# Reordering the first two tiles of a hybrid convolution and attention block

## The chip, the cores and the metric

The kernel runs on one core of one Trainium2 chip. The metric is the device time of one execution in microseconds (us), as the median of several runs; a separate execution is profiled. The core has five engines that each work through a queue of their own in order: PE (TensorE, matrix products; PEld is its weight load), DVE (VectorE), ACT (ScalarE), POOL (GpSimd) and SP (SyncE, which here issues nearly all DMAs).

## What is computed

One encoder layer over 4096 tokens of width 1024. A normalised input is projected by one large weight `w_in`; half of the columns feed a gated short convolution, the other half feed attention with three dilated windows, whose results are mixed and gated; a last projection is added to the input.

```python
h = rmsnorm(x, norm_w)
proj = jnp.einsum('bsd,de->bse', h, w_in)            # 1024 -> 4096
u, g_b, g_c, z_conv, q, k, v, z_attn = jnp.split(proj, splits, axis=-1)   # 512 columns each
y_conv = short_gated_conv(u, g_b, g_c, conv_w, conv_b) * jax.nn.silu(z_conv)
q = rmsnorm(q.reshape(b, s, ATTN_HEADS, HEAD_DIM), q_norm_w)
k = rmsnorm(k.reshape(b, s, ATTN_HEADS, HEAD_DIM), k_norm_w)
...   # three dilated windows, softmax over their log-sum-exps
y_attn = o.reshape(b, s, ATTN_WIDTH).astype(x.dtype) * jax.nn.silu(z_attn)
x = x + jnp.einsum('bse,ed->bsd', jnp.concatenate([y_conv, y_attn], axis=-1), w_out)
```

## The kernel before

The first stage, up to about 754 us, computes q, k, v and the attention gate z for 32 tiles of 128 tokens. Later stages do the convolution, the attention and the last projection. Products are exact to more than 16 bits: each operand is held as a high and a low half-precision part, and one product is three matmuls (high by high, high by low, low by high, lines 385 to 387).

The weights of q, k, v and z are the groups 4, 5, 6 and 7 of `w_in`, 512 columns each, held as 8 row blocks (kt) of 128 by 512. They arrive in float32 (`raw`) and are made into parts in the kernel, group by group:

- `w_square` (line 258, ACT) squares a block and sums each row; `w_scale` (lines 260 to 282) adds the eight sums, lets PE add across the partitions (line 264), takes an inverse root on POOL (line 267) and leaves one scale for the group;
- `w_split` writes the high part on ACT (line 286) and the low part on DVE (line 287).

Tokens go through `stats1` and `stats2` (the root mean square: ACT, POOL, then four small DVE steps) and then either `x_transpose` (PE turns the tile, lines 352 to 360) or `x_split` (parts on ACT and DVE, then two transposing DMAs issued by SP, lines 366 to 369). Before the change tiles 0, 1 and 2 take the first way, all others the second.

The first two tiles go together: `mm((0, 1), bank, group)` runs 48 matmuls, six for each row block. Functions given to `mm` by row block are issued between its matmuls, and that is where the squares, scales and splits of the next group stand, together with the later work on q and k: `post_qk1` (squares on ACT, sum on DVE, inverse root on POOL) and `post_qk2` (four small DVE steps, one or two products on DVE, a high part on ACT, a low part on DVE). `v_sums` adds the absolute values of v's weights (eight ACT steps and eight matmuls), `v_scales` and `v_gate` make factors of them that `post_v` and `post_z` need. From tile 2 on the loop `for t in range(2, NT)` handles one tile at a time; the order of the source is the order of every queue. Results of PE lie in eight banks; a bank can be written again when its last reader is done.

Of the kernel before, what the change touches and what calls it, by code (L numbers as in the profile page):

```python
# [65 lines left out]
def tile_hybrid_block(  # L66
# [39 lines left out]
    def bank(n, shape, dt=F32):  # L106
        return ps.tile(shape, dt, name=f"bank{n % 8}")
# [148 lines left out]
    def w_square(cg, kt, src):  # L256
        sq = pa.tile([128, D], F16, name="xsq")[:, 0:512]
        nc.scalar.activation(sq, src, AF.Square, scale=nwc[:, kt:kt + 1], accum_out=wss[:, cg, kt:kt + 1])

    def w_scale(cg):  # L260
# [12 lines left out]
        if cg in (4, 5):  # L273
            mul = 1.0 if cg == 4 else QK_SCALE
            c = rqs[:, cg - 4]
            nc.vector.tensor_scalar(c[:, 1:2], i, -0.5 * mul, None, op0=OP.mult)
            nc.vector.tensor_scalar(c[:, 2:3], i, 1.5 * mul, None, op0=OP.mult)
            nc.vector.tensor_scalar(c[:, 0:1], i, i, 1.0 / DH, op0=OP.mult, op1=OP.mult)
        if cg == 1:
            nc.vector.tensor_tensor(i, i, inv[:, 3:4], op=OP.mult)  # L280
        if cg in (3, 7):
            nc.vector.tensor_scalar(cz[:, cg // 4:cg // 4 + 1], i, 0.5, None, op0=OP.mult)

    def w_split(hi, lo, src, cg, kt):
# [4 lines left out]
    def group_steps(cg):  # L289
        def spl(kt):  # L290
            w = wa[(cg - 4) * 8 + kt]
            w_split(w[:, 0], w[:, 1], raw.pop((cg, kt)), cg, kt)
        return ([lambda kt=kt: w_square(cg, kt, raw[cg, kt]) for kt in range(KT)], [lambda: w_scale(cg)],
                [lambda kt=kt: spl(kt) for kt in range(KT)])

# [39 lines left out]
    def stats1(t):  # L335
        sq = pa.tile([128, D], F16, name="xsq")
        ss = pa.tile([128, 1], F32, name="ssx", bufs=2)
        nc.scalar.activation(sq, XT[t], AF.Square, accum_out=ss)
        RX[t] = rsqrt1(ss, 1, 1.0 / D, "x")

    def stats2(t):
        RX[t] = rsqrt2(RX[t], -0.5 * H_SCALE, 1.5 * H_SCALE)

    def h_views(t):
        c = t // 2
        b = (hb[c] if t % 2 else h_room(c, c % 3))[:, t % 2]
        HT[t] = (b[:, 0], b[:, 1])
        return HT[t]

    def x_transpose(t, b0=4):  # L350
        hi, lo = h_views(t)
        nc.vector.tensor_scalar(XT[t], XT[t], RX.pop(t), None, op0=OP.mult)
        for g in range(2):
            p = bank(b0 + g, [128, 4, 128])
            for k in range(4):
                kt = 4 * g + k
                nc.tensor.transpose(p[:, k, :], XT[t][:, kt * 128:(kt + 1) * 128], identf)
            s = slice(4 * g, 4 * g + 4)
            nc.scalar.activation(hi[:, s], p, AF.Copy)
            nc.vector.tensor_tensor(lo[:, s], p, hi[:, s], op=OP.subtract)  # L360
# [14 lines left out]
    def h_store(c):  # L375
        nc.sync.dma_start(hT_d[c], hb.pop(c).rearrange("p a b k n -> p (a b k n)"))
# [68 lines left out]

    vs = pa.tile([128, 512], F32, name="vs")

    def v_sums():
        pcs = bank(7, [128, 512])
        for n in range(KT):  # L450
            a = pa.tile([128, 512], F16, name="wk", bufs=3)
            nc.scalar.activation(a, wa[16 + n][:, 0], AF.Abs)
            nc.tensor.matmul(pcs, ones16, a, start=n == 0, stop=n == KT - 1)
        nc.vector.tensor_scalar(vinv, pcs, 1e-30, None, op0=OP.max)

    def v_scales():
# [49 lines left out]
        nc.vector.tensor_scalar(cvec, cq[:, 2, :], cm[:, 1:2], QK_SCALE, op0=OP.mult, op1=OP.mult)  # L506


    steps = {cg: group_steps(cg) for cg in (4, 5, 6, 7)}
    cq = pa.tile([128, 3, DH], F32, name="cq")  # L510
    nc.sync.dma_start(cq[:, 0, :], dap(q_norm_w, 0, [[0, 128], [1, DH]]))
    nc.sync.dma_start(cq[:, 1, :], dap(k_norm_w, 0, [[0, 128], [1, DH]]))
    stats1(0)
    stats1(1)
    stats2(0)
    stats2(1)
    x_transpose(0, 4)
    x_transpose(1, 6)
    for part in steps[4]:
        run_tasks(part)  # L520

    def with_steps(cg, more=None):
        sq, fin, spl = steps[cg]
        out = {kt: [] for kt in range(KT)}
        for kt in range(4):
            out[kt] += sq[2 * kt:2 * kt + 2]
        out[3] += fin
        for kt in range(4):
            out[4 + kt] += spl[2 * kt:2 * kt + 2]
        for kt, tasks in (more or {}).items():  # L530
            out[kt] += tasks
        return out

    pq = mm((0, 1), 0, 4, with_steps(5), 4)
    pk = mm((0, 1), 2, 5, with_steps(6, {
        0: [lambda: post_qk1(0, "q", pq[0])], 1: [lambda: post_qk1(1, "q", pq[1])], 2: [gains],
        5: [lambda: post_qk2(0, "q")], 7: [lambda: post_qk2(1, "q")]}))
    pv = mm((0, 1), 4, 6, with_steps(7, {
        0: [lambda: post_qk1(0, "k", pk[0]), lambda: qk_store(0, "q")], 1: [lambda: post_qk1(1, "k", pk[1])],
        2: [lambda: qk_store(1, "q"), v_sums], 3: [lambda: stats1(2)], 4: [v_scales, lambda: stats2(2)],  # L540
        5: [lambda: post_qk2(0, "k"), lambda: x_transpose(2, 0)], 6: [lambda: post_qk2(1, "k")], 7: [v_gate]}))
# [728 lines left out]
```

## Time and profile before

| | us |
|---|---|
| median of 3 runs (2233.95 to 2235.58) | 2235.02 |
| the profiled execution, its own time | 2230.64 |
| its span in the trace | 2228.8 |
| PE busy | 2109.8 (95% of the span) |
| DVE busy | 1432.0 (64%) |
| ACT busy | 1085.4 (49%) |

A row of the trace gives the start, the duration, the engine, the line, the operation and its operands, and in brackets how long the engine had sat idle and what ended that. Matmuls overlap, so the distance of two starts tells the pace, not the duration.

### The profile page before, as it was taken

The numbers are of one execution on the slowest core, as the hardware profiler recorded it, in microseconds if no ns is written. First come the engines' busy times: TensorE is split into PE (matmuls) and PEld (weight loads), VectorE is DVE, ScalarE is ACT, GpSimd is POOL, SyncE is SP. The second block draws the span as 40 slices with busy tenths as digits, with TensorE's granted clock in tenths as the row PEclk, the third lists the DMA queues.
The fourth block names the chain that finished last, engine by engine and source line by source line (L and its number), as shares of the span: only waits on it lengthen the run. The fifth ranks groups of instructions, "written<-read, shape, count | busy, mean of one in ns | idle before, by whom it ended". The sixth has DMA issues, their size and how long they took to land. (4 is left out here: it accounts for less than half of the span.)

```text
span 2228.8 us, 48736 instructions
## 1 busy us (share of the span) xinstructions
PE 2109.8 (95%) x17726; PEld 1559.6 (70%) x17726; DVE 1432.0 (64%) x4009; ACT 1085.4 (49%) x3128; POOL 844.9 (38%) x1635
## 2 busy tenths in 40 slices
PE   5699999999999989999999999999999899999999
PEld 2244444444444678888888898888888797788887
DVE  4655665655656346766666666676666676787776
ACT  6423333333333146766666666666666675222221
POOL 1123322232323255532554335553353354343332
PEclk9799999999999999999999999999999999999999
DMA  5155567775565586678865897668966458687775
GB/s 181 71 142 161 162 169 162 184 191 154 146 176 153 157 160 156 141 155 182 168 157 117 166 193 167 152 158 170 180 154 144 124 119 224 204 269 241 243 244 185
DMA packets 625006, 377.83 MB, mean 170 GB/s; under 512 B 401281, under 2 KB 567292, under 8 KB 618620
## 3 DMA queue, kind: packets, MB, share of 16 engines
q1 hardware_dynamic: 503396, 304.19, 55.1%
q10 hardware_dynamic: 121368, 70.53, 12.5%
q8 instruction: 139, 2.28, 0.4%
q14 instruction: 103, 0.84, 0.1%
HBM read 174.54 MB, written 110.39 MB: 128 GB/s over the span
## 5 line engine op out<-in xcount | busy, mean ns | idle before, releaser
L809 PE MATMUL bank<-hb,w 128*128 128x256 f16 x2048 | 559.9, 273 | 0.1
L810 PE MATMUL bank<-hb,w 128*128 128x256 f16 x2048 | 559.9, 273 | 0.0
L811 PE MATMUL bank<-hb,w 128*128 128x256 f16 x2048 | 559.8, 273 | 0.0
L387 PE MATMUL bank<-wa,hb 128*128 128x512 f16 x1024 | 392.5, 383 | 6.0 <-DMA hb<-xs 6.0
L385 PE MATMUL bank<-wa,hb 128*128 128x512 f16 x1024 | 393.0, 384 | 2.1 <-ACT wa L286 2.1
L386 PE MATMUL bank<-wa,hb 128*128 128x512 f16 x1024 | 392.5, 383 | 0.2 <-DVE wa L287 0.2
L1013 DVE CUSTOM_DVE_ANT_0 L<-bank,bt,alpha 128x256 f32<-128x256 f32 (+1 forms) x768 | 319.2, 453 | 106.9 <-PE bank L1001 79.3
L1022 ACT ACTIVATE L<-L,ot 128x256 f32<-128x256 f32 (+1 forms) x768 | 363.6, 476 | 25.9 <-DVE ot L1013 24.7
L238 POOL TENSOR_TENSOR rs_rq<-rs_mq,mhalf 128x8 f32<-128x8 f32 x64 | 107.8, 1684 | 301.1 <-DVE rs_mq L237 301.1
L974 POOL COPY qz<-qk 64x128 f16<-64x128 f16 x512 | 158.4, 309 | 161.3 <-PE bank L1001 143.9
L811 PEld LDWEIGHTS <-w 128*128 128x128 f16 x2048 | 201.0, 98 | 23.7
L810 PEld LDWEIGHTS <-w 128*128 128x128 f16 x2048 | 201.0, 98 | 22.2 <-issue 0.3
L809 PEld LDWEIGHTS <-w 128*128 128x128 f16 x2048 | 201.0, 98 | 19.8
L1057 DVE SCALAR_TENSOR_TENSOR pt<-bank,pt 128x512 f16<-128x512 f32 x192 | 132.6, 691 | 118.9 <-ACT pt L1045 118.5
L1045 ACT ACTIVATE pt<-bank 128x512 f16<-128x512 f32 x192 | 114.6, 597 | 169.0 <-PE bank L1039 163.8
L387 PEld LDWEIGHTS <-hb 128*128 128x128 f16 x1024 | 101.1, 99 | 132.6 <-DMA hb<-xs 8.9
L1076 PE MATMUL bank<-vt,pt 128*128 128x64 f16 x1536 | 175.7, 193 | 19.2 <-DMA pt<-src 16.6
L1061 DVE SCALAR_TENSOR_TENSOR src<-L,src 128x384 f16<-128x384 f32 (+1 forms) x192 | 131.2, 683 | 92.0 <-ACT src L1051 85.6
L385 PEld LDWEIGHTS <-hb 128*128 128x128 f16 x1024 | 102.1, 100 | 124.3 <-issue 7.2
L386 PEld LDWEIGHTS <-hb 128*128 128x128 f16 x1024 | 101.2, 99 | 124.2 <-issue 7.4
L1077 PE MATMUL bank<-vt,pt 128*128 128x64 f16 x1536 | 175.9, 193 | 0.0
L1078 PE MATMUL bank<-vt,pt 128*128 128x64 f16 x1536 | 175.9, 193 | 0.0
(197 smaller groups left out, 4478.4 us busy)
## 6 DMA issues: line engine op xcount, KB each, us to landing
hb<-hT SPq DMA_DIRECT2D x32, 1024.0 KB, 5.6
o_d<-ot ACTq DMA_DIRECT2D x32, 528.0 KB, 5.1
qk<-o_d SPq DMA_DIRECT2D x63, 264.0 KB, 3.6
hT<-hb SPq DMA_DIRECT2D x16, 1024.0 KB, 4.1
wst<-in_w_in_dram SPq DMA_DIRECT2D x64, 256.0 KB, 2.8
qk<-in_x_dram SPq DMA_DIRECT2D x32, 512.0 KB
qk_d<-h SPq DMA_DIRECT2D x128, 96.0 KB, 3.6
vt<-v_d ACTq DMA_DIRECT2D x48, 256.0 KB, 4.2
```

Of the source, the lines that this page charges most:

```text
L385: nc.tensor.matmul(p, hi[:, kt, :], w[:, 0], start=kt == 0, stop=False)
L386: nc.tensor.matmul(p, hi[:, kt, :], w[:, 1], start=False, stop=False)
L387: nc.tensor.matmul(p, lo[:, kt, :], w[:, 0], start=False, stop=kt == KT - 1)
L809: nc.tensor.matmul(pt, w_h, hi[:, :, kt], start=kt == 0, stop=False)
L810: nc.tensor.matmul(pt, w_h, lo[:, :, kt], start=False, stop=False)
L811: nc.tensor.matmul(pt, w_l, hi[:, :, kt], start=False, stop=kt == KT - 1)
L974: nc.gpsimd.tensor_copy(QZ[u % QZB][i][half], cols(q_t[i], U["qc"], half))
L1013: nc.vector.tensor_tensor_reduce(out=L[:, i], in0=p[i][:, 0:kn], in1=bias[:, U["b0"]:U["b0"] + kn], scale=alpha, scalar=BIG, op0=OP.add, o ...
L1022: nc.scalar.activation(L[:, i], L[:, i], AF.Exp, scale=-1.0, bias=ot[:, b, i, DH:DH + 1], accum_out=ot[:, b, i, DH + 1:DH + 2])
L1076: nc.tensor.matmul(p[:, i], hi, v[:, 0:DH], start=j == 0, stop=False)
L1077: nc.tensor.matmul(p[:, i], hi, v[:, DH:], start=False, stop=False)
L1078: nc.tensor.matmul(p[:, i], lo, v[:, 0:DH], start=False, stop=j == 1)
```

## The change

All that moves lies in the first stage's work on tiles 0, 1 and 2. The scale of each group is now made from four squares on ACT and four maxima of absolute values on DVE (`square`, `w_max`) in place of eight squares, and three short DVE steps join them. The squares of the next group stand between the splits of the present one. The work of tiles 0 and 1 on q and k stands behind all splits, in the matmuls of z; so do the absolute values of v's weights, into tiles of their own, while the matmuls that add them stand behind q of tile 2, in bank 1. Tile 2 goes the way of the later tiles, by transposing DMAs. z of tiles 0 and 1 goes to the banks 6 and 7.

```diff
+    def w_max(cg, kt, src):
+        nc.vector.tensor_reduce(wss[:, cg, kt:kt + 1], src, axis=AX.X, op=OP.max, apply_absolute_value=True)
+    def w_scale(cg, maxima=0):
+        if maxima:
+            t = wss[:, cg, KT - maxima:]
+            nc.vector.tensor_tensor(t, t, nwc[:, KT - maxima:], op=OP.mult)
+            nc.vector.tensor_tensor(t, t, t, op=OP.mult)
...
+    def square(cg, n):
+        w_square(cg, n, raw[cg, n])
+        w_max(cg, n + 4, raw[cg, n + 4])
...
     stats1(0)
+    stats2(0)
+    xp0 = x_transpose(0, 4)
     stats1(1)
-    stats2(0)
+    x_parts(0, xp0)
     stats2(1)
-    x_transpose(0, 4)
-    x_transpose(1, 6)
-    for part in steps[4]:
-        run_tasks(part)
+    xp1 = x_transpose(1, 6)
+    for n in range(4):
+        square(4, n)
+        if n == 1:
+            x_parts(1, xp1)
+    w_scale(4, 4)
...
+    def parts(cg):
+        out = [each(spl, cg, kt) for kt in range(KT)]
+        if cg < 7:
+            for n, at in enumerate((3, 5, 7, 9)):
+                out.insert(at, each(square, cg + 1, n))
         return out
+    run_tasks(parts(4))
+    pq = mm((0, 1), 0, 4, {5: [each(w_scale, 5, 4)], 7: parts(5)})
+    pk = mm((0, 1), 2, 5, {5: [each(w_scale, 6, 4)], 7: parts(6)})
+    pv = mm((0, 1), 4, 6, {5: [each(w_scale, 7, 4)], 7: parts(7) + [
+        each(stats1, 2), gains, each(post_qk1, 0, "q", pq[0]), each(stats2, 2)]})
     load_x(3)
     load_x(4)
+    pz = mm((0, 1), 6, 7, {
+        0: [each(x_split, 2)], 1: [each(post_qk2, 0, "q"), each(post_qk1, 1, "q", pq[1])],
+        2: [each(qk_store, 0, "q"), v_abs], 3: [each(post_qk2, 1, "q"), each(post_qk1, 0, "k", pk[0])],
+        4: [each(qk_store, 1, "q"), each(stats1, 3)], 5: [each(post_qk2, 0, "k"), each(post_qk1, 1, "k", pk[1])],
+        6: [each(qk_store, 0, "k"), each(stats2, 3)], 7: [each(post_qk2, 1, "k"), each(h_store, 0)]})
...
     pq = mm((2,), 0, 4)[0]
+    qk_store(1, "k")
+    v_sums()
+    v_scales()
+    post_v(0, pv[0])
+    post_v(1, pv[1])
+    v_gate()
     post_z(0, pz[0])
     post_z(1, pz[1])
```

The removed calls of `mm` had the same matmuls, with squares, scale and splits of the next group at fixed row blocks and the work on q, k and v in between.

ACT before, at the end of the squares of v's weights (`w_191` and the like are blocks of raw weights, `wa_..` their parts, `h_..` the parts of q, `wk` a scratch tile):

```order
L258 ACTIVATE xsq,wss<-w_195,nwc 128x512
L258 ACTIVATE xsq,wss<-w_197,nwc 128x512
L286 ACTIVATE wa_125<-w_183,nws 128x512
L286 ACTIVATE wa_126<-w_185,nws 128x512
L286 ACTIVATE wa_127<-w_187,nws 128x512
L286 ACTIVATE wa_128<-w_189,nws 128x512
L416 ACTIVATE h_531<-wk 128x4x2x64
L286 ACTIVATE wa_129<-w_191,nws 128x512
```

ACT after the change, in the second half of the splits of k's weights:

```order
L295 ACTIVATE wa_119<-w_170,nws 128x512
L258 ACTIVATE xsq,wss<-w_183,nwc 128x512
L295 ACTIVATE wa_120<-w_172,nws 128x512
L258 ACTIVATE xsq,wss<-w_185,nwc 128x512
L295 ACTIVATE wa_121<-w_174,nws 128x512
L258 ACTIVATE xsq,wss<-w_187,nwc 128x512
L295 ACTIVATE wa_122<-w_176,nws 128x512
L258 ACTIVATE xsq,wss<-w_189,nwc 128x512
L295 ACTIVATE wa_123<-w_178,nws 128x512
```

Four squares of v's weights stand singly between the splits of k's, and no step on q (`h_531`) stands among them any more.

PE before, in the matmuls of v (bank 4 and 5), where the turning of tile 2 stands (`hb3` holds the tile, `hb0` the turned tiles 0 and 1):

```order
L387 MATMUL bank5_566<-wa21_130,hb0_255 128x512
L357 MATMUL bank0_715<-identf_93,hb3_144 128x128 x4
L357 MATMUL bank1_722<-identf_93,hb3_144 128x128 x4
L385 LDWEIGHTS hb0_255
L385 MATMUL bank4_565<-wa22_131,hb0_255 128x512
```

PE after the change, behind q of tile 2 (`w6`, `w7` hold absolute values of v's weights, `hb1` the turned tile 2):

```order
L475 MATMUL bank1_829<-w6_696,ones16_220 128x512
L475 LDWEIGHTS ones16_220
L475 MATMUL bank1_829<-w7_698,ones16_220 128x512
L401 LDWEIGHTS hb1_646
L401 MATMUL bank1_891<-wa8_117,hb1_646 128x512
L402 LDWEIGHTS hb1_646
```

The sum of v's weights and k of tile 2 now follow each other in the same bank 1, and nothing in v's matmuls waits for tile 2.

DVE before, where that sum is read (`vinv`):

```order
L401 TENSOR_REDUCE ssq_601<-wk_599 128x8
L237 TENSOR_SCALAR rs_mq_603<-ssq_601,rqs_224 128x8
L454 TENSOR_SCALAR vinv_141<-bank7_621 128x512
L262 TENSOR_REDUCE wtot_657<-wss_223 128x1
L265 TENSOR_SCALAR wtot_657<-bank7_659 128x1
```

DVE after the change:

```order
L425 TENSOR_TENSOR wk_793<-bank3_435,rs_rq_764 128x512
L433 TENSOR_TENSOR h16_795<-wk_793,h16_795 128x4x128
L476 TENSOR_SCALAR vinv_141<-bank1_829 128x512
L479 RECIPROCAL vs_225<-vinv_141 128x512
L480 TENSOR_SCALAR vs_225<-vs_225 128x512
```

The read of the sum moved from before the splits of z's weights to behind the last step on k of tile 1 (`h16_795`).

## Rows read from the trace of the kernel before

**Rows 1.** Stretches: busy time (instructions) by engine, granted clock, DMA share, GB/s.
```profile
63.00:93.20 30.20, 10.18 (x37) 4.36 (x36) 16.95 (x38) 16.71 (x35) 5.52 (x5) 0.67 0.16 54
93.20:134.30 41.10, 41.10 (x184) 18.28 (x182) 23.21 (x51) 13.07 (x22) 10.33 (x9) 0.95 0.35 114
134.30:2228.80 2094.50, 2022.43 (x17374) 1520.48 (x17372) 1360.63 (x3835) 1014.04 (x2988) 822.58 (x1609) 0.99 0.70 173
```

**Rows 2.** Waits of PE, 0 to 135 us: total us, times, longest.
```profile
PE bank L357 <- DVE hb L352: 12.6, 2, 10.6
PE bank L264 <- DVE wtot L262: 12.2, 3, 7.6
PE bank L453 <- ACT wk L452: 9.4, 1, 9.4
```

**Rows 3.** Timeline from the first tile to the first matmul of q.
```profile
5.88 0.57 POOL L238 TENSOR_TENSOR rs_rx<-rs_mx,mhalf 128x1 f32<-128x1 f32 x1 [4.81 <-DVE rs_mx L237]
...
9.49 0.75 DVE L352 TENSOR_SCALAR xt<-xt,rs_rx 128x1024 f32<-128x1024 f32 x1
...
10.29 1.97 PE L357 MATMUL bank<-identf,xt 128*128 128x128 f32 x8 [10.29 <-DVE xt L352]
11.45 0.60 ACT L359 ACTIVATE hb<-bank 128x512 f16<-128x512 f32 x1 [3.47 <-PE bank L357]
...
16.84 0.71 ACT L258 ACTIVATE xsq<-w,nwc 128x512 f16<-128x512 f32 x1
...
23.60 0.16 DVE L262 TENSOR_REDUCE wtot<-wss 128x1 f32<-128x8 f32 x1 [5.93 <-ACT xsq L258]
...
25.78 5.01 ACT L286 ACTIVATE wa<-w,nws 128x512 f16<-128x512 f32 x8 [2.21 <-DVE nws L269]
...
26.54 5.39 DVE L287 SCALAR_TENSOR_TENSOR wa<-w,nws,wa 128x512 f16<-128x512 f32 x8 [0.17 <-ACT wa L286]
26.55 0.58 PE L385 MATMUL bank<-wa,hb 128*128 128x512 f16 x1 [2.09 <-ACT wa L286]
```

**Rows 4.** Timeline of PE: two starts at each pace.
```profile
30.71 0.63 PE L385 MATMUL bank<-wa,hb 128*128 128x512 f16 x1
...
31.13 0.63 PE L386 MATMUL bank<-wa,hb 128*128 128x512 f16 x1
...
33.39 0.38 PE L385 MATMUL bank<-wa,hb 128*128 128x512 f16 x1
...
33.61 0.38 PE L386 MATMUL bank<-wa,hb 128*128 128x512 f16 x1
```

**Rows 5.** Stretch right after the longest wait, columns as in rows 1.
```profile
93.20:97.00 3.80, 3.80 (x11) 1.37 (x9) 3.43 (x9) 1.85 (x4) 0.00 (x0) 0.50 0.16 52
```

**Rows 6.** Timeline: q of tile 2, its later work, and the parts of tile 3.
```profile
113.47 0.60 ACT L399 ACTIVATE wk<-bank 128x512 f32<-128x512 f32 x1 [4.43 <-PE bank L387]
113.96 1.14 ACT L366 ACTIVATE xs<-xt,rs_rx 128x1024 f16<-128x1024 f32 x1
114.10 0.69 DVE L401 TENSOR_REDUCE ssq<-wk 128x8 f32<-128x512 f32 x1 [4.34 <-ACT wk L399]
...
115.12 2.73 SPq L369 DMA_TRANSPOSE hb<-xs  x2
115.13 1.65 POOL L238 TENSOR_TENSOR rs_rq<-rs_mq,mhalf 128x8 f32<-128x8 f32 x1 [3.39 <-DVE rs_mq L237]
115.13 1.28 DVE L367 SCALAR_TENSOR_TENSOR xs<-xt,rs_rx,xs 128x1024 f16<-128x1024 f32 x1
...
117.74 0.69 DVE L409 TENSOR_TENSOR wk<-bank,rs_rq 128x512 f32<-128x512 f32 x1
...
119.19 0.63 ACT L416 ACTIVATE h<-wk 128x512 f16<-128x512 f32 x1 [4.09 <-DVE wk L412]
```

**Rows 7.** The line of the transposing DMAs: from issue to landing.
```profile
DMA to landing us min/median/max: 4.1/4.3/4.4
```

**Rows 8.** Timeline: the reciprocal of v's sums.
```profile
81.70 3.35 DVE L457 RECIPROCAL vs<-vinv 128x512 f32<-128x512 f32 x1
```

**Rows 9.** Timeline: ACT takes q of tile 3 when its last matmul ends.
```profile
134.32 0.60 ACT L399 ACTIVATE wk<-bank 128x512 f32<-128x512 f32 x1 [4.28 <-PE bank L387]
```

More of the change, by code (lines that the diff above doesn't have):

```diff
@@ L258, in w_square @@
         nc.scalar.activation(sq, src, AF.Square, scale=nwc[:, kt:kt + 1], accum_out=wss[:, cg, kt:kt + 1])
-    def w_scale(cg):
+    def w_max(cg, kt, src):
[5 more added lines that the diff above has]
+            nc.vector.tensor_tensor(t, t, t, op=OP.mult)
         tot = pa.tile([128, 2], F32, name="wtot", bufs=2)
@@ L287, in w_split, with spl @@
         nc.vector.scalar_tensor_tensor(lo, src, s, hi, op0=OP.mult, op1=OP.subtract)
[L289 to L294, printed above, removed]
+    def spl(cg, kt):
+        w = wa[(cg - 4) * 8 + kt]
+        w_split(w[:, 0], w[:, 1], raw.pop((cg, kt)), cg, kt)
+    def square(cg, n):
+        w_square(cg, n, raw[cg, n])
+        w_max(cg, n + 4, raw[cg, n + 4])
     wc = [[[None] * 4 for _ in range(4)] for _ in range(2)]
@@ L350, in x_transpose @@
     def x_transpose(t, b0=4):
-        hi, lo = h_views(t)
         nc.vector.tensor_scalar(XT[t], XT[t], RX.pop(t), None, op0=OP.mult)
+        out = []
         for g in range(2):
@@ L357, in x_transpose, with x_parts @@
                 nc.tensor.transpose(p[:, k, :], XT[t][:, kt * 128:(kt + 1) * 128], identf)
+            out.append(p)
+        return out
+    def x_parts(t, banks):
+        hi, lo = h_views(t)
+        for g, p in enumerate(banks):
             s = slice(4 * g, 4 * g + 4)
@@ L446, in tile_hybrid_block, with v_abs @@
     vs = pa.tile([128, 512], F32, name="vs")
+    VA = []
+    def v_abs():
+        for n in range(KT):
+            VA.append(wpool.tile([128, 512], F16, name=f"w{n}"))
+            nc.scalar.activation(VA[n], wa[16 + n][:, 0], AF.Abs)
     def v_sums():
-        pcs = bank(7, [128, 512])
+        pcs = bank(1, [128, 512])
         for n in range(KT):
-            a = pa.tile([128, 512], F16, name="wk", bufs=3)
-            nc.scalar.activation(a, wa[16 + n][:, 0], AF.Abs)
-            nc.tensor.matmul(pcs, ones16, a, start=n == 0, stop=n == KT - 1)
+            nc.tensor.matmul(pcs, ones16, VA[n], start=n == 0, stop=n == KT - 1)
         nc.vector.tensor_scalar(vinv, pcs, 1e-30, None, op0=OP.max)
@@ L506, in gains @@
         nc.vector.tensor_scalar(cvec, cq[:, 2, :], cm[:, 1:2], QK_SCALE, op0=OP.mult, op1=OP.mult)
-    steps = {cg: group_steps(cg) for cg in (4, 5, 6, 7)}
     cq = pa.tile([128, 3, DH], F32, name="cq")
@@ L513, in tile_hybrid_block @@
     stats1(0)
+    stats2(0)
+    xp0 = x_transpose(0, 4)
     stats1(1)
-    stats2(0)
+    x_parts(0, xp0)
     stats2(1)
-    x_transpose(0, 4)
-    x_transpose(1, 6)
-    for part in steps[4]:
-        run_tasks(part)
[L522 to L531, printed above, removed]
-        return out
@@ L534, in tile_hybrid_block @@
[L534 to L541, printed above, removed]
+    xp1 = x_transpose(1, 6)
@@ new lines, in tile_hybrid_block, with each @@
+    for n in range(4):
[3 more added lines that the diff above has]
+    w_scale(4, 4)
+    def each(f, *a):
+        return lambda: f(*a)
+    def parts(cg):
[3 more added lines that the diff above has]
+                out.insert(at, each(square, cg + 1, n))
+        return out
+    run_tasks(parts(4))
+    pq = mm((0, 1), 0, 4, {5: [each(w_scale, 5, 4)], 7: parts(5)})
+    pk = mm((0, 1), 2, 5, {5: [each(w_scale, 6, 4)], 7: parts(6)})
@@ L542, in tile_hybrid_block @@
+    pv = mm((0, 1), 4, 6, {5: [each(w_scale, 7, 4)], 7: parts(7) + [
+        each(stats1, 2), gains, each(post_qk1, 0, "q", pq[0]), each(stats2, 2)]})
     load_x(3)
     load_x(4)
-    pz = mm((0, 1), 2, 7, {
-        0: [lambda: qk_store(0, "k"), lambda: post_v(0, pv[0])], 1: [lambda: qk_store(1, "k"), lambda: post_v(1, pv[1])],
-        2: [lambda: h_store(0), lambda: stats1(3)], 4: [lambda: stats2(3)]})
+    pz = mm((0, 1), 6, 7, {
[3 more added lines that the diff above has]
+        6: [each(qk_store, 0, "k"), each(stats2, 3)], 7: [each(post_qk2, 1, "k"), each(h_store, 0)]})
```

## The prediction

> **What bounds the kernel now.** Read first the stretches of time [rows 1]. From 134.3 us to the end PE is busy for 2022 of 2094 us: whatever comes earlier shifts the rest with it, one for one, if nothing else in the first stage waits. From 93.2 to 134.3 PE never stops. From 63.0 to 93.2 it works for only 10 of 30 us, and no other engine is full there either: that is queueing, not work. The list of PE's waits says for what [rows 2]: 10.6 us at once for tile 2 to be scaled (its turning stands in the middle of v's matmuls), 9.4 us for the absolute values of v's weights, and 12.2 us for three group scales. Before that, the first matmul of q starts only at 26.55 us [rows 3]. So some 22 + 20 us of start-up are idle PE, and the change aims at both.
>
> I measure the result at one event, the end of q of tile 3: ACT takes that bank at 134.32 us [rows 9]. The question is when that event comes after the change.
>
> **Step 1, the first scale: 4.6 us earlier.** Before, eight squares run from 16.84 to 23.60 us, 0.845 us each, behind all four evictions of the turned tiles. After, ACT does four, DVE four maxima. Chain: POOL's root for tile 0 is done at 6.45 us [rows 3]; its four small steps now stand ahead of tile 1's and take some 0.8 us, so scaling starts at 7.3 instead of 9.49, turning at 8.1, the first eviction at 9.1 (1.16 us later, as 10.29 to 11.45). Two evictions with their low parts end at 11.8, tile 1's small steps and scaling at 13.4, its evictions, with the maxima around them, at 17.1, two more maxima at 18.5. Three small joining steps of about 0.2 us follow: the sum that started at 23.60 starts at 19.0.
>
> No row shows a maximum over 512 columns. The nearest is the DVE sum over 512 columns, 0.69 us [rows 6], the same elements read once, and I take it; the upper bound is a DVE pass over twice the elements, 1.28 us [rows 6]. Below 0.69 I allow 0.4, worth half a microsecond here.
>
> **Step 2, q of tiles 0 and 1.** From sum to first matmul 2.95 us [rows 3], so PE starts at 22.0. Before, the first matmuls ran at a distance of 0.43 us and from 32.0 on at 0.216 [rows 4]: the lower level (1.2 GHz) for 5.4 us, then the upper (2.4 GHz). I keep that stretch: 0.3 us wait for the first low part, 13 matmuls in 5.4 us, and 23 more at 0.216 take PE past row block 5, where k's scale stands, at 32.5 us. The splits (0.63 us on ACT, 0.67 on DVE [rows 3]) and k's squares between them are done by 31: PE is what ends last in this group.
>
> **Step 3, k and v.** In each period DVE does eight splits and four maxima, 8 x 0.67 + 4 x 0.69 = 8.2 us; around them 2.7 us from a scale's sum to its first low part, 0.6 us for the joining steps, and about 0.2 of waiting for ACT, which holds a square (0.85) between two splits. That is 11.7 us. PE's 48 matmuls and the scale's own take 10.75. So DVE and ACT set the period, PE waits 0.9 us in each, and the scale of v is at 44.2, that of z at 55.9 us. Behind the latter PE has 12 matmuls of v and 48 of z: z ends at 69.2 us. The old place of the 10.6, 9.4 and 7.6 us waits is gone: the squares cost nothing as long as the splits of the same period cover them.
>
> **Step 4, what is late next.** Everything on q, k and v now forms one line on DVE behind the last split, which ends at 63.7 us. First tile 2: its square, the gains (seven steps), the sum of q, four small steps; parts on ACT and DVE of 1.14 and 1.28 us [rows 6]; two DMAs, issued at 68.4 and 69.8, landing 4.3 us later [rows 7]. PE, done at 69.2, gets tile 2 in full only at 74.1: a new wait of nearly 5 us. q of tile 2 ends at 79.4 and the eight sum matmuls at 81.1.
>
> Then comes the dearest piece. k of tile 2 wants bank 1, which holds the sum until DVE reads it, and that read stands behind four rounds of later work. One round is, from [rows 6]: four small steps 0.9, one or two products of 0.69, a high part on ACT 0.63, the next square on ACT 0.55, the sum 0.69, a small step 0.3, POOL 1.65 and some hand-overs. No round overlaps the next on DVE: 6.5 us for each of the first two, 5.8 for the third, 3.1 for what the fourth still has to do. From 69.7 (behind tile 2's low part) that is 91.5, and with the read 92.2 us. So PE stands from 81.1 to 92.2: **an 11 us wait takes the place of those removed.** The eight absolute values (4.3 us on ACT) lie beside the second round and cost nothing.
>
> From 92.2, k, v and z of tile 2 take 3 x 24 x 0.216 = 15.5 us, to 107.7. Tile 3's parts are late too: DVE does the reciprocal, 3.35 us [rows 8], both v tiles (4.2), the gate (1.0), z (1.4); SP holds tile 3's two DMAs behind the stores of z, which wait for POOL. They are issued at 105.5 and 106.9, land by 111.2, and PE waits 3.5 us more. q of tile 3 ends at about 116.1 instead of 134.3.
>
> **Sum.** 134.3 - 116.1 = 18.2 us less. Of the profiled execution's own 2230.64 us (a span of 2228.8 and 1.8 around it) that leaves 2212.4; that execution lay 4.4 us under the median, so I set the forecast against the median: 2235.0 - 18.2 = 2216.8, about **2217 us**. Behind the event DVE needs about half of PE's time per tile (23 of 41 us in [rows 1]) and loses its backlog within two tiles.
>
> **The level of PE's clock.** After the 10.6 us wait the granted clock is 0.50 for 3.8 us, with 11 matmuls where the upper level has twice as many [rows 5]: about 1.8 us lost. After the change this falls to the waits at 69 and 81 us. The first loss lies inside the 11 us wait, the second delays PE from 107.7 to 109.5, still ahead of tile 3's landing. I charge nothing for either. The waits of 0.9 us within k and v have no equal before; if each brought such a stretch, DVE's 11.7 us period would hide half of it.
>
> **Rivals.**
>
> A. *PE stays at the lower level through the start-up (slower).* The place is k, v and z of tiles 0 and 1. At 0.427 us a matmul a group takes 20.5 + 0.4 us instead of the 11.7 us period, 9.2 us more; q's rest at that level costs 5 us. If q, k and half of v stay low, z's scale is at 79.4 instead of 55.9, the DVE line of step 4 follows it, and the event comes at 139.6: 2235.0 + 5.3 = 2240 us. It decides from two full groups on, 2 x 9.2 = 18.4. For it: the waits inside each group, and the low stretch in [rows 5]. Against: the stretch of [rows 5] follows 10.6 us of idleness, not 0.9, and here PE works 92% of each period. 4%.
> The Trainium skill's page TensorE: Matmul & The Clock Gate, section HAM oscillation, describes a kernel in which a wait between all bursts of matmuls puts the clock back to its lower level for every burst. By that rule the time would be rival A's; the stretch in [rows 5] agrees with the rule for a long wait, and no row shows it for 0.9 us.
>
> B. *The maxima are dear.* At 1.28 us the first scale comes 2.1 us later and the periods grow by 2 to 2.4 each once DVE is full: 6.6 us in all, 2223.5 us. No row speaks for a price above the sum's. 10%.
> The Trainium skill's page VectorE: DVE Perf Modes, section on the perf-mode tier table, gives such reductions one speed only, whatever the type; by it the price would be that of the sum, 0.69 us.
>
> C. *The DVE line is longer and eats the gain (no change).* If each of the four rounds and the v steps met one more engine hand-over of 3 to 4 us, for instance ACT held by the absolute values or POOL by its copies of k, the bank would come free at 108 and the event at 132: 2230 to 2235 us. For it: these are in-order queues with four engines in each round. Against: each step's row is known, and ACT is free half of the time there. 7%.
>
> D. *Tile 3 lands in time,* because SP's queue moves faster than I have it: no wait at 107.7, 2213 us. 14%; my forecast itself, 2212 to 2222, has 65%.
>
> **How the numbers follow.** 2217 is the likeliest case. The range 2209 to 2227 takes in B and D, and a round more or less of step 4; A and most of C lie outside. Faster by over 0.2% (about 4.5 us, what a measurement of this kernel tells from no change): the forecast, B, D and a little of C, 0.89; within 0.2%: most of C, 0.07; slower: A, 0.04.
>
> **What would show it.** The first scale's sum near 19 and the first matmul near 22 us; scales about 11.7 us apart; PE idle about 5 us before q of tile 2 and about 11 before k of tile 2, ended by the DVE read of v's sums; no PE wait for a scaled tile 2; ACT taking q of tile 3 near 116 us; PE full behind it. I would be wrong if the scales lay 14 us or more apart (B), if the matmuls of k and v ran at 0.43 us (A), if bank 1 came free past 100 us (C), or if the later part of the first stage lost time that it does not lose now.

## The result

The changed kernel takes 2221.63 us in the median of five runs, the kernel before 2233.95 beside it: a ratio of 0.9931 (95% interval 0.9909 to 0.9953), 12 us faster where 18 were forecast. In a second set of six runs it took 2214.69, against 2233.64: 0.9913 (0.9892 to 0.9935). Over all runs the mean is 2216.8 us (11 runs, standard error 1.5) against 2234.1 (83 runs, 0.4), a gain of 17.3; two runs of the kernel before, at 2745.35 and 5472.58 us, are left out. The other runs of one kernel lie up to 18 us apart.

The profiled execution took 2221.63 us, with a span of 2219.8 (2228.8 before). The same stretches as in [rows 1], same columns:

```profile
63.00:93.20 30.20, 15.90 (x65) 6.35 (x64) 20.66 (x48) 10.31 (x18) 9.36 (x7) 0.83 0.30 96
93.20:134.30 41.10, 40.10 (x186) 17.87 (x185) 27.65 (x61) 14.29 (x24) 16.03 (x12) 1.00 0.50 141
134.30:2219.80 2085.50, 2009.91 (x17274) 1515.74 (x17271) 1346.93 (x3809) 1007.35 (x2978) 816.67 (x1605) 0.99 0.70 172
```

In the first stretch PE works 15.9 us instead of 10.2. Of the 14.3 us in which it idles there, 12.05 are one wait. PE's waits from 0 to 140 us, to be held against [rows 2]:

```profile
PE bank L401 <- DVE vinv L476: 12.1, 1, 12.1
...
PE bank L273 <- DVE wtot L271: 3.4, 1, 3.4
...
PE bank L401 <- DVE wk L425: 1.5, 1, 1.5
PE bank L403 <- DMA hb<-xs: 0.9, 2, 0.7
PE bank L401 <- DMA hb<-xs: 0.8, 1, 0.8
```

The waits for a scaled tile 2 in the middle of v (10.6 us) and for the absolute values (9.4) are gone, and of the 12.2 us for scales only the first scale's 3.4 is left. In their place stands the bank-1 wait. The timeline of the changed kernel, with the steps of the prediction in order (start, duration, engine, line, operation; in brackets the idle time before and what ended it):

```profile
12.69 1.27 DVE L263 TENSOR_REDUCE wss<-w 128x1 f32<-128x512 f32 x2
...
17.84 0.16 DVE L271 TENSOR_REDUCE wtot<-wss 128x1 f32<-128x8 f32 x1
...
20.79 0.58 PE L401 MATMUL bank<-wa,hb 128*128 128x512 f16 x1 [2.09 <-ACT wa L295]
...
31.84 0.28 PE L273 MATMUL bank<-wtot,ones 128*128 128x1 f32 x2
...
42.62 0.38 PE L273 MATMUL bank<-wtot,ones 128*128 128x1 f32 x2
...
53.49 0.38 PE L273 MATMUL bank<-wtot,ones 128*128 128x1 f32 x2
...
65.58 2.68 SPq L385 DMA_TRANSPOSE hb<-xs  x2
...
68.54 0.38 PE L401 MATMUL bank<-wa,hb 128*128 128x512 f16 x1 [1.49 <-DVE wk L425]
...
88.03 0.68 DVE L476 TENSOR_SCALAR vinv<-bank 128x512 f32<-128x512 f32 x1
...
88.76 0.59 PE L401 MATMUL bank<-wa,hb 128*128 128x512 f16 x1 [12.05 <-DVE vinv L476]
...
102.16 3.35 SPq L385 DMA_TRANSPOSE hb<-xs  x2
...
106.80 0.39 PE L401 MATMUL bank<-wa,hb 128*128 128x512 f16 x1 [0.78 <-DMA hb<-xs]
...
112.17 0.38 PE L403 MATMUL bank<-wa,hb 128*128 128x512 f16 x1
...
114.51 0.63 ACT L450 ACTIVATE h<-wk 128x512 f16<-128x512 f32 x1 [2.42 <-DVE wk L448]
...
115.62 0.59 ACT L415 ACTIVATE wk<-bank 128x512 f32<-128x512 f32 x1
...
154.08 0.60 ACT L415 ACTIVATE wk<-bank 128x512 f32<-128x512 f32 x1 [3.15 <-PE bank L403]
```

The event of the prediction is ACT's 115.62 (116.1 forecast, 134.32 before). But that row has no wait in brackets: PE ended q of tile 3 at 112.4, and ACT came to it 3 us later. The steps on v and z of tile 2 stand ahead of it in ACT's queue, and for 2.42 of these 3 us ACT sat idle until DVE had scaled v of tile 2 (row at 114.51): DVE is behind, and ACT passes that on. The first q for which ACT again waits for PE, in the same way as in [rows 9], is that of tile 5: 154.08 here, 175.69 before, **21.6 us ahead**. I use that row below as well. The same steps of ACT, held side by side, stay 20 to 22 us ahead up to 1010 us (21.4 there) and end 9.0 ahead. The loss lies between 1010 and 1680 us, in the attention stage, whose code did not change.

### The profile page after: what moved, and what is told of

Read it like the earlier page. It is cut to its first block, busy times and chain, and to the rows that moved or that the text cites. A ratio compares the mean times of both kernels' runs of the same rounds, so it can differ in the third digit from the quotient of the medians.

```text
span 2219.8 us, 48689 instructions
## 1 busy us (share of the span) xinstructions
PE 2112.3 (95%) x17718; PEld 1561.8 (70%) x17718; DVE 1440.1 (65%) x4031; ACT 1071.0 (48%) x3095; POOL 846.4 (38%) x1635
## 5 line engine op out<-in xcount | busy, mean ns | idle before, releaser
L402 PEld LDWEIGHTS <-hb 128*128 128x128 f16 x1024 | 100.9, 99 | 135.4 <-issue 18.1
```

Source lines behind the costliest of these rows:

```text
L402: nc.tensor.matmul(p, hi[:, kt, :], w[:, 1], start=False, stop=False)
```

## The experiments

Two questions: which part of the change brings the 21.6 us, and what takes part of them back a thousand microseconds later. In this table, PE's own matmuls of the scales are the marks; all times are us of one profiled execution each.

| kernel | first scale | scale of z | q of tile 3 (ACT) | q of tile 5 | z's scale to q of tile 5 |
|---|---|---|---|---|---|
| before | 23.9 | 77.9 | 134.3 | 175.7 | 97.8 |
| changed | 18.2 | 53.5 | 115.6 | 154.1 | 100.6 |
| changed, again | 18.0 | 53.3 | 115.5 | 153.5 | 100.2 |
| eight squares | 18.9 | 60.7 | 122.8 | 160.9 | 100.2 |
| old first steps | 22.1 | 57.3 | 119.5 | 157.7 | 100.3 |
| squares behind splits | 18.1 | 52.2 | 114.3 | 152.4 | 100.2 |
| q's rounds early | 18.2 | 63.6 | 115.8 | 156.1 | 92.5 |
| tile 3 forward | 18.2 | 52.2 | 114.4 | 152.4 | 100.3 |
| ... and vinv read early | 18.1 | 52.4 | 115.6 | 154.6 | 102.2 |
| ... and rounds overlapped | 18.2 | 52.6 | 115.4 | 153.3 | 100.8 |
| ... and absolute values split | 18.1 | 52.7 | 112.9 | 150.5 | 97.9 |

### One part undone or alone

**Eight squares** instead of four squares and four maxima:

```diff
-        w_max(cg, n + 4, raw[cg, n + 4])
+        w_square(cg, n + 4, raw[cg, n + 4])
...
-    w_scale(4, 4)
+    w_scale(4)
... (and so for the scales of groups 5, 6 and 7)
```

> The changed kernel with eight squares on ACT for each group's scale in place of four squares and four maxima; the order stays. Theory (the maxima take ACT's half of the scale off the period): ACT then has 8 x 0.63 + 8 x 0.85 = 11.8 us a group and the chain through the scale besides, the scales come 13 to 14 us apart instead of 10.9, the first scale's sum at 21 instead of 17.8, and ACT takes q of tile 3 at 124 to 127 instead of 115.6. Rival (order and the freed places alone brought the gain, the squares lie beside other work): event at 119 or sooner.

Measured: median 2225.95 us, 0.9968 of before (0.9954 to 0.9983). The event comes at 122.8 us, 1.2 us ahead of the range for the theory and far from the rival's. PE now waits for each scale:

```profile
32.95 0.38 PE L273 MATMUL bank<-wtot,ones 128*128 128x1 f32 x2 [1.32 <-DVE wtot L271]
46.83 0.38 PE L273 MATMUL bank<-wtot,ones 128*128 128x1 f32 x2 [1.66 <-DVE wtot L271]
60.70 0.38 PE L273 MATMUL bank<-wtot,ones 128*128 128x1 f32 x2 [1.66 <-DVE wtot L271]
```

The scales lie 13.9 us apart instead of 10.9, as the theory said; the first scale is only 0.8 us later, not 3, which fits gaps of ACT there that the further squares fill. The maxima are worth 7 us.

**Old first steps**: the small steps and the turning of tiles 0 and 1 in the order of before.

```diff
-    stats2(0)
-    xp0 = x_transpose(0, 4)
     stats1(1)
-    x_parts(0, xp0)
+    stats2(0)
     stats2(1)
-    xp1 = x_transpose(1, 6)
+    x_parts(0, x_transpose(0, 4))
+    x_parts(1, x_transpose(1, 6))
...
-        if n == 1:
-            x_parts(1, xp1)
```

> The changed kernel with the first steps in the order of before: both tiles' small steps first, then both turnings with their parts, then the squares and maxima of q's weights. Theory (PE, DVE and ACT keep their period behind the first scale, so that the start is carried one for one): the first scale's sum at 21.7 us as in the kernel before with maxima, instead of 17.8, and ACT takes q of tile 3 at 119 to 120. Rival (DVE's line behind the splits has slack that takes up the delay): event at 116 to 117.

Measured: event 119.5, q of tile 5 at 157.7, both 3.6 to 4.2 us later than in the two profiles of the changed kernel; the first sum, at 21.82 us, is 4.0 later. The start is carried one for one, as the theory said. (Median 2216.08; differences of that size drown in the scatter of whole runs.)

**Squares behind the splits**, which takes away the regular order of squares and splits:

```diff
-            for n, at in enumerate((3, 5, 7, 9)):
-                out.insert(at, each(square, cg + 1, n))
+            out += [each(square, cg + 1, n) for n in range(4)]
```

> The changed kernel with the four squares and four maxima of the next group behind the eight splits of the present one, instead of one pair between each two of them. Theory (in each period DVE is full: 8 splits and 4 maxima are 8.2 us of its work in whatever order, and ACT's four squares lie beside the maxima): the scales of v and z again 10.9 us apart, at most 11.2, and ACT takes q of tile 3 within 0.7 us of 115.6 and q of tile 5 within 0.7 of 154. Rival (the regular order itself makes the period, since four squares of 0.85 us at the end would be waited for): scales 11.8 to 12.5 us apart, q of tile 5 at 156 or later.

```profile
30.41 0.28 PE L273 MATMUL bank<-wtot,ones 128*128 128x1 f32 x2
41.24 0.38 PE L273 MATMUL bank<-wtot,ones 128*128 128x1 f32 x2
52.17 0.38 PE L273 MATMUL bank<-wtot,ones 128*128 128x1 f32 x2
```

Periods of 10.8 and 10.9 us, the same as with the regular order, and a median of 2216.42. The theory holds in that the order does not make the period, and ACT's squares cost nothing behind the splits either. That DVE's sum of work alone sets it is not shown: PE's 48 matmuls and the scale's take 10.75 us (48 at 0.216 and the scale's row), nearly the same. (The 1.4 us by which all marks are earlier come from the first matmuls, see the last section.)

**The maxima alone**, in the kernel before:

```diff
-        return ([lambda kt=kt: w_square(cg, kt, raw[cg, kt]) for kt in range(KT)], [lambda: w_scale(cg)],
+        return ([lambda n=n: square(n) for n in range(4)], [lambda: w_scale(cg, 4)],
... (w_max, the joining steps and square as in the change, one square and one maximum by row block)
```

> The kernel before with nothing but the scales made of four squares and four maxima; order, places and the turning of tile 2 stay. Theory (each piece takes away what stood ahead of its own wait): the first scale's sum near 20.2 instead of 23.60, and tile 2 scaled on DVE 7 to 10 us sooner than at 90.3; ACT takes q of tile 3 at 124 to 128 instead of 134.3. Rival (in the old order DVE's line is what tile 2 waits for, and 28 maxima of 0.68 us on it eat the gain): event at 131 or later.

Measured: median 2224.35, 0.9963 (0.9952 to 0.9974); event at 128.3. That is 6.1 us, 0.3 us outside the range of the theory and clearly not the rival's. The first sum comes at 21.72, not 20.2; with the old first steps in the changed kernel it comes at 21.82, so the order of the first steps holds it back. PE's timeline shows where the rest went:

```profile
65.41 4.22 PE L463 MATMUL bank<-wk,ones 128*128 128x512 f16 x8 [7.30 <-ACT wk L462]
85.23 1.97 PE L367 MATMUL bank<-identf,hb 128*128 128x128 f32 x8 [10.57 <-DVE hb L362]
```

The wait for tile 2 is still 10.57 us, as in [rows 2]; the turning behind it starts at 85.23 us where it started at 91.49.

**Tile 2 by DMA alone**, in the kernel before:

```diff
-        5: [lambda: post_qk2(0, "k"), lambda: x_transpose(2, 0)], 6: [lambda: post_qk2(1, "k")], 7: [v_gate]}))
+        5: [lambda: post_qk2(0, "k"), lambda: x_split(2)], 6: [lambda: post_qk2(1, "k")], 7: [v_gate]}))
```

> The kernel before with nothing but tile 2 taken by transposing DMAs instead of being turned by PE, from the same place in v's matmuls. Theory (the 10.6 us wait hides the next one: z of tile 1 goes to bank 3, which k of tile 1 holds until its product on DVE at 97.0): the wait for a scaled tile 2 goes, PE stops instead for bank 2 or 3 in z until 89 to 96 us, and ACT takes q of tile 3 at 129 to 133 instead of 134.3. Rival (the whole 10.6 us is saved): event near 124.

```profile
PE bank L453 <- ACT wk L452: 11.1, 1, 11.1
...
PE bank L385 <- DVE wk L409: 10.0, 2, 5.6
```

The 10.6 us wait is gone from PE's list, and 10.0 us for the banks of k stand in its place (two waits, 5.58 us ahead of z at 90.1 us and 4.41 at 96.0). The event moves by 0.9 us, q of tile 5 by 0.9, and the median is 2240.04, 1.0032 of before (1.0017 to 1.0046), so slower over the whole run. By itself this part is worth nothing. The new wait is the theory's; the event, at 133.4, lies 0.4 us behind its range.

**q's rounds early**: the later work on q of tiles 0 and 1 back in front of z's scale.

```diff
-    pk = mm((0, 1), 2, 5, {5: [each(w_scale, 6, 4)], 7: parts(6)})
+    pk = mm((0, 1), 2, 5, {5: [each(w_scale, 6, 4)], 7: parts(6)[:8]
+        + [each(post_qk1, 0, "q", pq[0])] + parts(6)[8:] + [each(post_qk1, 1, "q", pq[1])]})
+    pv = mm((0, 1), 4, 6, {2: [gains, each(post_qk2, 0, "q")], 4: [each(post_qk2, 1, "q")], ...
... (the same steps taken out of z's matmuls, k's moved up)
```

> The changed kernel with the later work on q of tiles 0 and 1 back in front of z's scale and splits (its squares and sums around the splits of v, its products in v's matmuls, with the gains); only k's two rounds stay behind all splits. Theory (the length of DVE's line counts, where q's rounds stand in it does not): z's scale comes 7 to 9 us later than 53.5, the bank-1 wait shrinks by as much, vinv is read at 83 to 88, and ACT takes q of tile 3 at 112 to 117 against 115.6. Rival (to have all splits first is what the change lives from): event at 121 or later.

The rows of PE's wait for z's scale, and of the read that frees bank 1:

```profile
63.63 0.58 PE L273 MATMUL bank<-wtot,ones 128*128 128x1 f32 x2 [10.16 <-DVE wtot L271]
...
88.18 0.68 DVE L476 TENSOR_SCALAR vinv<-bank 128x512 f32<-128x512 f32 x1
```

z's scale comes 10 us later and PE waits 10.16 us for it, and yet vinv is read at 88.18 instead of 88.03 and the event comes at 115.8 instead of 115.6. The wait has only changed its place. q of tile 5 comes 2.0 to 2.7 us later than in the two profiles of the changed kernel, the median is 2220.39. To have all splits first is worth 2 to 3 us, by that row; mostly the length of the line on DVE decides. And of these 2 to 3 us some 1.5 go with a stretch at half the clock that falls into q and k of tile 3 here:

```profile
108.60:112.10 3.50, 3.50 (x10) 1.27 (x9) 1.48 (x5) 0.47 (x1) 1.87 (x2) 0.52 0.28 80
```

10 matmuls start in 3.5 us, where the pace of 0.216 makes 16. The theory's range for the read (83 to 88) is missed by 0.2 us, its event (112 to 117) is met.

### Trying to shorten what is late next

**Tile 3 forward**: its parts and DMAs right behind the read of vinv.

```diff
     v_sums()
+    x_split(3)
     v_scales()
...
-        if t + 1 < NT:
+        if 2 < t < NT - 1:
             x_split(t + 1)
```

> The changed kernel with the parts and DMAs of tile 3 issued right behind the read of v's sums, ahead of the reciprocal, both v tiles, the gate and z. Theory (two late things in series: the bank-1 wait to 88.8 us, then tile 3's DMAs, issued at 102.2 us behind the stores of z): k of tile 2 starts at 88.8 as now, tile 3 lands near 97, the wait of PE ahead of q of tile 3 goes, and ACT takes q of tile 3 at 110 to 112 instead of 115.6, some 4 us gained. Rival (tile 3 was landing in time anyway, or v and z of tiles 0 and 1 hold banks 4 to 7 instead): 115 or later.

PE's waits there, first of this kernel, then of the next:

```profile
PE bank L401 <- DVE vinv L476: 10.6, 1, 10.6
```

```profile
PE bank L401 <- DMA hb<-xs: 8.2, 1, 8.2
PE bank L401 <- DVE vinv L476: 3.2, 1, 3.2
```

The wait for tile 3 is gone, but it had been only 1.0 us, not the 3.5 of the prediction, and from z's scale to q of tile 5 it takes 100.3 us, as in the changed kernel: this theory fell. Its lead of 1 to 1.7 us was there at z's scale already. (Median 2212.89, 0.9911 of before, 0.9890 to 0.9931.)

**vinv read early as well**: both rounds on k behind the read.

```diff
... (both rounds on k taken out of z's matmuls)
+    v_sums()
+    post_qk2(0, "k")
+    post_qk1(1, "k", pk[1])
+    qk_store(0, "k")
+    x_split(3)
+    post_qk2(1, "k")
     qk_store(1, "k")
-    v_sums()
     v_scales()
```

> As the kernel with tile 3 moved forward, and besides both rounds of later work on k of tiles 0 and 1 stand behind the read of v's sums instead of ahead of it, so that bank 1 comes free when the sums end. Theory: k of tile 2 starts at 82 instead of 88.8, nothing waits for tile 3 at 97, ACT takes q of tile 3 at 105 to 107, some 9 us ahead of the changed kernel, and the median falls by as much, less what the attention stage scatters. Rival (the length of DVE's line decides, whatever its order: v of tile 2 waits for bank 2, q of tile 3 for bank 4 until v of tile 0 is scaled): the waits of PE move to those banks and the event comes at 111 or later.

Bank 1 is free at 80.3 us and its wait falls to 3.2, but PE then loses 8.2 us at tile 4, whose parts stand behind the whole backlog of DVE and ACT. The two together are about what the bank cost alone, and z's scale to q of tile 5 takes 102.2. The event, at 115.6, is the rival's, but the wait has moved to the parts of tile 4 and not to the banks 2 and 4 that the rival names. The median, 2215.65, is no better than 2214.69.

**Rounds overlapped**, then besides five of the absolute values ahead of z's splits:

```diff
-        1: [each(post_qk2, 0, "q"), each(post_qk1, 1, "q", pq[1])],
+        1: [each(post_qk1, 1, "q", pq[1]), each(post_qk2, 0, "q")],
```

(and so for the other rounds, with tile 3 forward)

> As the kernel with tile 3 moved forward, and in z's matmuls the first half of the next round on q and k (square, sum, small step, POOL's root) stands ahead of the second half of the present one. The bank-1 wait did not shorten the idle time when the read of v's sums was moved ahead of the rounds on k: PE then lost 8.2 us to tile 4 instead, so the length of DVE's line decides. Theory (the line is long because each round waits for POOL's root of 1.65 us and the hand-overs around it; in this order the roots lie beside the previous round): a round takes 4 to 4.5 us instead of 5.8 to 6.5, vinv is read at 82 to 83 instead of 86.7, PE waits some 6 us for bank 1 instead of 10.6, ACT takes q of tile 3 near 110 instead of 114.4, and the work at 260 us lies 27 us ahead of before instead of 23.3. Rival (DVE's own steps fill the line): vinv at 85.5 or later, the rest as with tile 3 moved forward.

```profile
69.67 4.25 ACT L470 ACTIVATE w<-wa 128x512 f16<-128x512 f16 x8
...
74.43 0.69 DVE L417 TENSOR_REDUCE ssq<-wk 128x8 f32<-128x512 f32 x1 [3.94 <-ACT wk L415]
```

vinv is read at 87.7 us, as late as the rival said, though not for its reason: DVE's line is not full, the absolute values now stand in front of a square that DVE waits 3.94 us for. (Median 2215.82.) The prediction's "lie beside the second round and cost nothing" is true only in the order for which it was said.

The second kernel besides:

```diff
-    pv = mm((0, 1), 4, 6, {5: [each(w_scale, 7, 4)], 7: parts(7) + [
+    pv = mm((0, 1), 4, 6, {5: [each(w_scale, 7, 4)], 7: [each(v_abs, 0, 5)] + parts(7) + [
... (and each(v_abs, 5, 8) in place of v_abs in z's matmuls)
```

> As the kernel with overlapped rounds and tile 3 moved forward, and five of the eight absolute values of v's weights stand ahead of z's splits, where ACT waits some 3 us for z's scale; three stay in z's matmuls. With overlapped rounds alone vinv was read at 87.7 us, no sooner: the absolute values (4.25 us on ACT) then stood in front of the square of k of tile 0, and DVE sat idle for 3.9 us behind them. Theory (that obstacle gone, the rounds take 4 to 4.5 us): vinv read at 82 to 84, PE's wait for bank 1 falls from 9.5 to 5 us or less, the work at 260 us lies 26 to 28 us ahead of before (22.4 with overlapped rounds alone, 23.3 with tile 3 alone). Rival (each gap that is closed opens the next one, as in the two tries before): vinv at 86 or later.

With the absolute values split, vinv is read at 85.15 us, between what theory and rival expected, and the whole from z's scale to q of tile 5 takes 97.9 us instead of 100.2: 2.3 to 2.9 us, the only gain of these four kernels in that measure, seen in one profile. The median is 2212.62, 0.9903 of before (0.9883 to 0.9923). That interval overlaps the changed kernel's, so no better kernel is shown.

### Where the gain is lost later

> The changed kernel, unaltered, profiled once more. In its first trace ACT takes q of tile 3 at 115.6 us (134.3 before), a gain of 18.7 us, and at 760 us the work lies 21.2 us ahead; at the end only 9. Theory (the loss in the attention stage is chance, from seven stretches of 3.4 us at granted clock 0.5 between 1020 and 1620 us where the trace of before has one): the event again at 115.6 within 0.3, but another number of such stretches, and with it another loss; five timed runs scattered over some 10 us, the best about 18 us under the best of before. Rival (the earlier start puts the attention stage into a worse rhythm): again six to eight stretches at nearly the same places, an end only 9 to 12 us ahead.

> The kernel before, unaltered, profiled once more. Theory of chance: the event again at 134.3 within 0.3 us; between 1000 and 1700 us some other number of stretches at granted clock 0.5 than the one seen, between none and seven, and a span that is longer by about 1.7 us for each further stretch. Rival (a rhythm that belongs to the kernel): again one stretch, or none.

The event is the same again, 115.5 us; with the kernel before it is 0.9 late, more than the 0.3 expected. In the attention stage the changed kernel shows five stretches of 3.4 us at half the clock where its first profile had seven, and before three where it had one (one of 6.8 us counts as two, here and below). The second profile ends 17.4 us ahead, as chance would have it; but all five stand within 8 us of a place where the first profile has one, as the rival says. What such a stretch is, in the first profile of the changed kernel (ahead, in it, behind):

```profile
1110.00:1126.20 16.20, 13.84 (x174) 12.44 (x173) 9.78 (x37) 9.19 (x35) 9.46 (x26) 1.00 0.55 160
1126.20:1129.60 3.40, 3.40 (x29) 2.74 (x27) 2.16 (x7) 2.75 (x11) 1.23 (x4) 0.50 0.71 160
1129.60:1133.00 3.40, 3.40 (x41) 3.14 (x40) 1.85 (x9) 1.02 (x4) 0.00 (x0) 1.00 0.34 77
```

PE had idled for 2.4 of 16 us, then the granted clock is 0.50 (1.2 GHz) for 3.4 us, then 1.00 again. Over all fourteen profiles (the two given and the twelve of the experiments), the time from q of tile 5 to the end goes with the number of such stretches in it:

| kernel | low stretches | rest, us | | kernel | low stretches | rest, us |
|---|---|---|---|---|---|---|
| before | 8 | 2053.2 | | vinv read early | 10 | 2058.9 |
| before, again | 11 | 2057.0 | | rounds overlapped | 6 | 2054.3 |
| maxima alone | 10 | 2053.4 | | absolute values split | 11 | 2058.0 |
| tile 2 by DMA alone | 11 | 2061.4 | | eight squares | 10 | 2057.9 |
| changed | 13 | 2065.8 | | q's rounds early | 13 | 2067.2 |
| changed, again | 12 | 2062.7 | | old first steps | 12 | 2061.7 |
| tile 3 forward | 9 | 2057.7 | | squares behind splits | 9 | 2056.8 |

A straight line through them costs each stretch 1.85 us, with a correlation of 0.84. The four kernels with the start of before have 8 to 11, the ten with the new start 6 to 13 (means 10 and 10.5): over the whole rest the number does not go with the change.

In the attention stage alone it does. Take two fixed steps of ACT in it, at 1010.0 and 1679.9 us in the kernel before, and the same two in every other profile. The stretches between them, before and changed, then before and changed a second time (columns as in [rows 1]):

```profile
1010.00:1679.90 669.90, 645.65 (x8001) 584.00 (x7998) 446.79 (x1504) 438.83 (x1514) 314.87 (x868) 1.00 0.77 162
988.60:1671.50 682.90, 654.77 (x8000) 590.10 (x7996) 447.14 (x1504) 438.72 (x1513) 312.43 (x868) 0.98 0.74 159
1012.20:1684.60 672.40, 648.96 (x8001) 585.73 (x7998) 447.18 (x1504) 438.53 (x1514) 313.77 (x868) 0.99 0.75 162
986.80:1667.00 680.20, 651.65 (x8000) 587.49 (x7997) 446.81 (x1504) 439.16 (x1514) 314.02 (x868) 0.99 0.73 160
```

Over all fourteen profiles the same work takes 667.0 to 675.3 us with the start of before (mean 671.2, with 2.25 low stretches) and 675.0 to 683.5 with the new start (mean 678.2, with 4.5): 7.0 us more. Outside these steps the new starts win some 3 us back. So the rival, that an earlier start puts the attention stage into a worse rhythm, is not refuted, and chance alone does not explain the loss. Of the 13 us by which the first pair differs here about half is the luck of that pair. Over the 11 and 83 runs the mean gain is 17.3 us where the start gains about 22, so that some 5 us are given back on average. Why the attention stage takes longer behind an earlier start stays open.

## Why the prediction was right, and where it was not

**Step 1** (first sum at 19.0): 17.84 us. A maximum costs 0.68 us, two in a row 1.27, the sum's price that I took. The chain came out 1.2 us shorter than my sum. Of the 5.8 us gained the order of the first steps brings 4.0 beside the maxima (old first steps: 21.82); the maxima bring 1.9 in the old order (21.72) and only 0.8 in the new one (eight squares: 18.60).

**Step 2** (first matmul at 22.0, k's scale at 32.5): 20.79 and 31.84. Right: the start carries the 1.2 us of step 1, and from there to k's scale it takes 11.05 us, not 10.5. But the granted clock does not bear out my reading of the slow first matmuls as the lower level: its record shows 1.00 there (last section).

**Step 3** (period 11.7, z's scale at 55.9): 10.9, and 53.5. The term that was mis-sized is DVE's work in a period: from v's sum at 42.40 to the first low part at 45.07 it takes the forecast 2.7 us, but splits, maxima and joining steps together take 8.2 up to z's sum at 53.28, not 9.0. PE's 0.9 us waits are not there: its own 10.75 us nearly fill the period.

**Step 4**: the round lengths were 6.4 and 5.6 us (6.5 and 5.8), by ACT's squares of the banks. The bank-1 wait is 12.05 us (11), ended by the read of vinv at 88.03 (91.5), which the earlier splits explain. Three terms were wrong. Tile 2 landed in time but for 0.7 us: its second DMA was issued at 67.0 instead of 69.8 and let PE go on 2.8 us later, where I had counted 4.3. So the 5 us wait for it became 1.49 us for bank 0, which the product of q still held and which I had not named. And PE waited 1.0 us for tile 3, not 3.5. Then DVE's backlog, which I had put behind the event, reached the event through ACT's queue and held it 3 us behind PE. The forecast of 116.1 was met at 115.6 because these misses cancelled, and that is luck: PE itself was nearly 4 us sooner than forecast.

**Carried one for one**: this is the step that failed. It holds up to 1010 us; then the attention stage takes 7.0 us longer on average behind the new start (13 in the profiled pair), and of the start's 22 us the runs keep three quarters, 17.3. I had looked for new waits in the first stage only, and treated the stage behind it as rigid. That the mean gain of 17.3 us lies so near the 18.2 of the forecast is luck too: the start gained more than forecast, and the stage behind it gave some back.

**Clock and rivals.** After the bank-1 wait the granted clock is 0.52 from 88.7 to 92.1 us, and the 72 matmuls of k, v and z of tile 2 start over 16.9 us (88.76 to 105.64) where the pace of 0.216 makes 15.3. That is 1.6 us lost; the forecast had the size right (1.8) and had hidden it behind tile 3. Behind the wait at 68.5 us no low stretch came. Rival A (low through the start-up) did not come, and the kernel with eight squares shows that more idle time did not bring it. There PE waits 1.3 to 1.7 us once a group and works 23 of 28 us:

```profile
33.00:61.00 28.00, 23.07 (x103) 9.89 (x104) 13.49 (x31) 22.17 (x48) 1.10 (x2) 1.00 0.01 2
```

The granted clock is 1.00 throughout. But the prediction was wrong to say that short waits within k and v have no equal before. The kernel before waits for its scales there, and each time a stretch at half the clock follows:

```profile
37.67 0.38 PE L264 MATMUL bank<-wtot,ones 128*128 128x1 f32 x2 [2.82 <-DVE wtot L262]
51.93 0.38 PE L264 MATMUL bank<-wtot,ones 128*128 128x1 f32 x2 [1.81 <-DVE wtot L262]
```

```profile
38.90:42.60 3.70, 3.70 (x11) 1.28 (x9) 3.42 (x11) 3.23 (x6) 0.00 (x0) 0.54 0.01 2
52.60:56.20 3.60, 3.60 (x10) 1.27 (x9) 2.42 (x7) 2.56 (x4) 0.55 (x1) 0.53 0.00 0
```

So waits of 2.82 and 1.81 us were followed by a low stretch, and those of 1.32 to 1.66 with eight squares were not; what parts them is not shown here. None of them held the clock low through a group, as rival A has it. The Trainium skill, TensorE: Matmul & The Clock Gate, section HAM oscillation, describes a kernel whose waits between all bursts of matmuls put the clock back each time. The wait of 12 us here and those of 2.82 and 1.81 us in the kernel before agree with it, the waits with eight squares do not.

B fell with the price of the maxima, C with vinv at 88.03. D was right in its mechanism, with 1.0 us of wait left, and PE's lead of 22 us at that place was D's.

The regular order of squares and splits brings nothing: squares between or behind the splits make the same period. The maxima (7 us), the order of the first steps (4 us) and q's rounds behind all splits (2 to 3 us) are some 13 of the 21.6, each taken from the whole change by itself. The remaining 8 were not taken apart. Probably they come from removing the old waits for tile 2, for v's absolute values and for z's scale together, and from the two low stretches above, which the changed kernel does not have; no run shows it, and removing the wait for tile 2 alone gave 0.9.

## What to carry to other kernels

Where several in-order engines work off a backlog together, the wait that is listed need not be the cost: take one away and the next engine or bank can wait as long (10.6 us for tile 2 became 10.0 for the banks of k). Compare the time from one fixed mark to the first row where the evicting engine again waits for PE. An early gain is not yet a gain of the whole run; see how a later stage scatters from run to run before its loss is given to the change, and look at it stage by stage before it is put down to chance.

## What was not expected of the hardware

**The first matmuls.** Each profile begins q at a distance of 0.43 us per matmul, and goes over to 0.216 at another time: at 24.4 us with the squares behind the splits, at 27.1 in the changed kernel, though both begin at 20.8. The record of the granted clock shows 1.00 on both sides of that point (of the changed kernel; in the kernel before it is 1.00 from 26.5 to 32.0 us as well):

```profile
21.50:27.10 5.60, 5.52 (x14) 1.89 (x14) 5.60 (x10) 5.60 (x13) 0.00 (x0) 1.00 1.05 387
27.10:31.80 4.70, 4.70 (x23) 2.23 (x22) 1.98 (x6) 0.75 (x2) 0.00 (x0) 1.00 1.03 362
```

14 matmuls in 5.6 us, then 23 in 4.7. Up to 1.4 us of a comparison of starts can be this.

**DVE beside POOL.** The same DVE step on a tile, 1.28 us in [rows 6], takes 2.30 in the one row in which it runs beside POOL's product for z:

```profile
98.31 2.51 POOL L458 TENSOR_TENSOR wk<-wk,vinv 128x512 f32<-128x512 f32 x2 [9.73 <-DVE wk L457]
99.59 2.30 DVE L383 SCALAR_TENSOR_TENSOR xs<-xt,rs_rx,xs 128x1024 f16<-128x1024 f32 x1
```

With tile 3 forward, where POOL does not work on z then, the same step takes 1.28 us again. The other rows of this step in the changed kernel take 1.27 to 1.29 us.
